# A decoder layer's ConvFFN: where modulation rows are fetched, how the first down weights are loaded, and the order at the turn of the down projection

## The chip, the core and the metric

The kernel runs on one core of one Trainium2 chip. The core has five engines, each with its own queue of instructions: TensorE (PE, matmuls; its weight loads are listed apart as PEld), VectorE (DVE), ScalarE (ACT), GpSimd (POOL) and SyncE (SP), which here only issues transfers. Sixteen DMA engines move data between HBM and the on-chip memory; transfers are issued by SP, by ACT and, for accumulating ones, by POOL. The metric is the device time of one execution in microseconds; lower is better.

## The reference

One layer on a sequence of 512 positions and 1024 channels in float32: a conditioned mixer (mLSTM heads and a Conformer convolution), then a conditioned ConvFFN. The change lies in the second half:

```
mod = silu(c) @ ada_w + ada_b          # six rows of 1024: sh1, sc1, g1, sh2, sc2, g2
...
u  = rms_norm(x, ffn_pre_g) * (1 + sc2) + sh2
up = causal_dwconv(u @ ffn_up, ffn_conv_w, ffn_conv_b)   # 1024 -> 2 * 2816, width 3
a, gt = split(up, 2)
f  = (silu(gt) * a) @ ffn_down                           # 2816 -> 1024
x  = x + g2 * rms_norm(f, ffn_post_g)
```

g2, the last of the modulation rows, is needed only at the end, and so its part of `mod` is computed late.

## The kernel before

**Products in two halves.** A float32 product is made of a high and a low half of each operand in the fast fp32r form: three matmuls, high by high, high by low, low by high (`mm3`, lines 188 to 190; `prod2`, line 1457). Halves are made in two ways. `split` lets ScalarE copy the high half (L1013) and VectorE subtract it (L1014). `added_split` (L1083 to L1085) lets ScalarE write the high half and its negative, and then GpSimd issues a software DMA that adds the source onto the negative, which leaves the low half: no VectorE work, but 256 KB of transfer with a landing to wait for. Halves live in a pool of 20 buffers, other tiles in 44 slots; raw weights arrive in two buffers of 128 x 2048 (`raws`), modulation rows in two of 128 x 1024 (`adas`).

**Up projection.** The 2816 gated channels are 22 blocks of 128 (`i`), taken in pairs, and a pair is one step `m`. From step 4 to step 10 (about 506 to 658 us) a step is one even block by a seven-product scheme of Strassen's kind (forms p1 to p7 of the weights' quarters, `weight_form`) and one odd block in the plain way, whose four quarters come from `value_part`, each an `added_split` (tiles wup_0, wup_1, wup_2, wup_3). Six quarter loads for the next step are issued by SP in the middle of a step. Steps 4 to 7 also fetch two blocks of modulation rows of 512 KB each on ACT's queue (`ada_fetch`) and sum them on VectorE against the conditioning vector (`ada_add`, L1148). `unit_out` multiplies the value by the gate into `F`.

**Down projection.** The same scheme, over 11 row blocks. Phase 1 (about 658 to 720 us) forms p1, p5, p7 and p6 from `b1`, `t1`, `t3`, `t2` (`load1`, `forms1`, `part_b`, `parts1`, `prod1`; `fh` and `fl` are the halves of the activations, in part reloaded from HBM). `b1` of the first blocks, and of the last three, is made by `added_split` (`part_b`), other halves by `split`. `t2` goes out to HBM and is read again. Then comes the turn: VectorE adds p6 and p1 into `su`, `su` into p5 and p7, and p7 into `sp5`, and TensorE goes on in the same banks with phase 2 (720 to 767 us), p2, p3 and p4, from `b2`, `b4`, `t4` (`load2`, `forms2`, `prod2`) and from the other activations `g2` (`forms_g2`). At the end the rows are normalised, scaled and written.

**What sets the order.** A scheduler orders each engine's instructions by what is ready; inside an `in_order()` block ScalarE, VectorE and GpSimd keep the order in which the code is written. SP's and TensorE's orders follow the code as well. Phase 1 and the up steps stand in such a block; phase 2 before the last products doesn't. There `behind_turn` keeps VectorE forms behind the instruction in `turn`, while `held` is true. A transfer waits on its issuing queue until its buffer is free, and holds up those behind it.

## Time and profile before

| what | value |
|---|---|
| timed runs | 773.89, 773.82, 771.59 us (median 773.82) |
| profiled execution | 775.42 us |
| its span, first to last instruction | 773.7 us |
| mean granted TensorE clock | 0.995 |
| TensorE busy | 755.8 us (98%) |
| VectorE busy | 643.5 us (83%) |
| ScalarE busy | 451.9 us (58%) |
| GpSimd busy | 370.8 us (48%) |
| bytes moved | 149.52 MB, 193 GB/s in the mean |

In the rows of a profile a matmul is busy until its modelled end, so that successive matmuls overlap: the distance of two starts, not the duration, is what one costs. A row of waits gives who waited, for whom, the total in us, how often, and the longest. A row of a tile gives the line, engine and operation, how many, the shortest, median and longest duration in ns, and the first and last start in us; "DMA to landing" is from issue to arrival. Names lose their numbers there: `p` stands for p1 to p7, `sp` for sp1 and sp5, `b_2l` for the low half of b1, b2 or b4 of block 2, `t_2l` likewise.

### The profile page before, as it was taken

The page shows a single profiled execution, that of the slowest core. Times are in us where ns is not written, and L with a number is a line of the kernel's source. Part 1 is how long each engine was busy: PE and PEld are TensorE (multiplying, and loading weights), DVE is VectorE, ACT ScalarE, POOL GpSimd, SP SyncE. Part 2 cuts the span into 40 slices and gives each one's busy share as a digit, 9 for nine tenths or more (in the row PEclk, how much of TensorE's full clock was granted, in tenths as well). Part 3 has the DMA queues.
Part 4 walks back from the last instruction along what each step waited for, and adds up shares of the span by engine and source line. Part 5 has one row for each costly group of instructions (what it writes and reads, how often), then busy time and mean ns, then how long its engine had stood idle before and what let it go on. Part 6 is the DMA issues. An engine that isn't in the chain of part 4 may idle for free.

```text
span 773.7 us, 11565 instructions
## 1 busy us (share of the span) xinstructions
PE 755.8 (98%) x3961; PEld 645.0 (83%) x3961; DVE 643.5 (83%) x1030; ACT 451.9 (58%) x864; POOL 370.8 (48%) x324
## 2 busy tenths in 40 slices
PE   7999999999999999999999999999998999899996
PEld 5888898778888888988889988899987989788785
DVE  6987999999999867746858589879898768996996
ACT  5447266776676356671344566676665657656662
POOL 2039587696797644452851445465555643100001
PEclk9999999999999999999999999999999999999998
DMA  9983214123031552436953678889988787999872
GB/s 328 383 287 133 84 55 170 75 74 118 28 116 75 168 194 75 164 108 226 346 189 143 186 190 208 244 214 238 219 210 201 173 235 185 283 361 359 315 259 108
DMA packets 56575, 149.52 MB, mean 193 GB/s; under 512 B 6434, under 2 KB 7874, under 8 KB 52420
## 3 DMA queue, kind: packets, MB, share of 16 engines
q1 hardware_dynamic: 33588, 100.37, 37.5%
q10 hardware_dynamic: 14288, 32.68, 12.2%
q0 software_dynamic: 8640, 15.73, 11.6%
q8 instruction: 31, 0.51, 0.3%
q14 instruction: 28, 0.23, 0.1%
HBM read 117.42 MB, written 15.61 MB: 172 GB/s over the span
## 4 chain that ended last, share of the span: by engine, by line
PE 52%; DVE 26%; DMA 13%; ACT 3%; issue 3%; POOL 1%; ACTq 0%; SPq 0%; DVEq 0%; POOLq 0%
DVE cv L731 10%; PE up L190 5%; PE up L189 5%; PE up L188 5%; PE p L1457 4%; PE glu L190 3%; PE glu L188 3%; PE glu L189 3%; DMA fh_1b<-own 2%; PE glu L316 2%; PE mixa L188 2%; PE mixa L190 2%; PE mixa L189 2%; PE mixb L190 2%; PE mixb L189 2%
## 5 line engine op out<-in xcount | busy, mean ns | idle before, releaser
L731 DVE SCALAR_TENSOR_TENSOR cv<-gt,cvw,cv 128x505 f32<-128x505 f32 (+24 forms) x200 | 137.3, 729 | 2.3 <-ACT cv L719 1.1
L727 POOL TENSOR_TENSOR cs<-cs,cs 128x510 f32<-128x510 f32 (+3 forms) x32 | 41.9, 1308 | 0.3
L725 ACT ACTIVATE cs<-gt,cvw 128x511 f32<-128x511 f32 (+4 forms) x40 | 27.4, 716 | 6.4 <-POOL cs L727 3.2
L685 POOL TENSOR_TENSOR ro2r<-ro2t,mhalf 128x1 f32<-128x1 f32 x1 | 0.6, 561 | 53.1 <-DVE ro2t L683 53.1
L189 PE MATMUL up<-u2l,wup_0h 128*128 128x512 f32 (+1 forms) x72 | 25.7, 356 | 0.2 <-DVE u2l L910 0.2
L188 PE MATMUL up<-u2h,wup_0h 128*128 128x512 f32 (+1 forms) x72 | 25.6, 356 | 0.0
L190 PE MATMUL up<-u2h,wup_0l 128*128 128x512 f32 (+1 forms) x72 | 25.5, 354 | 0.0
L171 POOL TENSOR_TENSOR wglu_0l<-wglu,wglu_0h 128x512 fp32r<-128x512 f32 x4 | 5.6, 1396 | 40.4 <-ACT wglu_0h L170 40.4
L171 POOL TENSOR_TENSOR wqko_1024l<-wqko,wqko_1024h 128x512 fp32r<-128x512 f32 x12 | 15.5, 1290 | 18.3 <-ACT wqko_1024h L170 12.9
L155 DVE SCALAR_TENSOR_TENSOR junk<-spare,cb 128x1024 bf16<-128x1024 f32 x12 | 19.0, 1586 | 3.6 <-DMA spare<-in_adaT 3.4
L155 DVE SCALAR_TENSOR_TENSOR junk<-ada,cb 128x1024 bf16<-128x1024 f32 x12 | 18.8, 1570 | 3.7 <-DMA ada<-in_adaT 3.6
L188 PE MATMUL qko<-uh,wqko_1024h 128*128 128x512 f32 x48 | 20.6, 430 | 0.0
L190 PE MATMUL up<-u2h,wup_2l 128*128 128x512 f32 x44 | 17.9, 408 | 2.7 <-DMA wup_2l<-wups 2.7
L188 PE MATMUL qko<-uh,wqko_0h 128*128 128x512 f32 x48 | 20.2, 420 | 0.0
L276 DVE SCALAR_TENSOR_TENSOR junk<-ada,cb 128x1024 bf16<-128x1024 f32 x16 | 19.5, 1220 | 0.1
L171 POOL TENSOR_TENSOR wo_512l<-wo,wo_512h 128x512 fp32r<-128x512 f32 x8 | 12.9, 1615 | 13.7 <-ACT wo_512h L170 13.7
L171 POOL TENSOR_TENSOR wqko_0l<-wqko,wqko_0h 128x512 fp32r<-128x512 f32 x12 | 16.6, 1386 | 5.0 <-ACT wqko_0h L170 4.9
L190 PE MATMUL qko<-uh,wqko_1024l 128*128 128x512 f32 x48 | 18.8, 392 | 0.0
L190 PE MATMUL qko<-uh,wqko_0l 128*128 128x512 f32 x48 | 18.8, 391 | 0.0
L171 POOL TENSOR_TENSOR wqko_512l<-wqko,wqko_512h 128x512 fp32r<-128x512 f32 x12 | 17.0, 1416 | 3.7 <-ACT wqko_512h L170 3.7
L171 POOL TENSOR_TENSOR wo_1024l<-wo,wo_1024h 128x512 fp32r<-128x512 f32 x8 | 11.6, 1454 | 14.9 <-ACT wo_1024h L170 14.9
L189 PE MATMUL qko<-ul,wqko_1024h 128*128 128x512 f32 x48 | 18.7, 390 | 0.0
(1247 smaller groups left out, 3136.9 us busy)
## 6 DMA issues: line engine op xcount, KB each, us to landing
wups<-in_w_up SPq DMA_DIRECT2D x56, 256.0 KB, 5.3
wqko<-in_w_qko SPq DMA_DIRECT2D x12, 1024.0 KB, 4.8
ada<-in_adaT ACTq DMA_DIRECT2D x20, 512.0 KB, 5.7
ada<-in_adaT SPq DMA_DIRECT2D x16, 512.0 KB, 6.8
wo<-in_w_out SPq DMA_DIRECT2D x8, 1024.0 KB, 4.8
wup<-in_w_up SPq DMA_DIRECT2D x8, 1024.0 KB, 6.1
spare<-in_adaT ACTq DMA_DIRECT2D x12, 512.0 KB, 7.4
wd<-in_w_down SPq DMA_DIRECT2D x20, 256.0 KB, 5.8
```

Source lines behind the costliest of these rows:

```text
L155: t = V.scalar_tensor_tensor(out=junk, in0=r, scalar=1.0, in1=cb, op0=ALU.mult, op1=ALU.mult, accum_out=mod[:, i : i + 1])
L171: (eng or G).tensor_tensor(out=lo[:, :n], in0=src, in1=hi[:, :n].bitcast(F32), op=ALU.subtract)
L188: PE.matmul(ps, a[0], b[0], start=start, stop=False)
L189: PE.matmul(ps, a[0], b[1], start=False, stop=False)
L190: PE.matmul(ps, a[1], b[0], start=False, stop=stop)
L276: V.scalar_tensor_tensor(out=junk, in0=first[k][:, i * D : (i + 1) * D], scalar=1.0, in1=cb, op0=ALU.mult, op1=ALU.mult, accum_out=part[k] ...
L316: PE.matmul(banks0[i], blk(wk, i)[a], u[k][b], start=k == 0 and a == b, stop=False)
L685: G.tensor_tensor(out=r, in0=t, in1=mhalf[:, :1], op=ALU.pow)
L725: S.activation(t[:, d:], cvx[j][:, : T - d], AF.Copy, scale=w(CK - 1 - d))
L727: G.tensor_tensor(out=side[:, d:], in0=side[:, d:], in1=t[:, d:], op=ALU.add)
L731: last_tap[0] = V.scalar_tensor_tensor(out=cp[:, d:], in0=cvx[j][:, : T - d], scalar=w(CK - 1 - d), in1=cp[:, d:], op0=ALU.mult, op1=ALU.add)
L1457: PE.matmul(ps[q], x, y, start=False, stop=m == NM - 1 and i == 2, skip_group_check=True)
```

## The change

Three things are done.

*Modulation rows.* `ada_fetch` goes from the step's start (behind the form p3, ahead of the six loads of quarters) to the place behind `value_part(j + 2, 0)`. Both `ada_add` go behind `unit_out`, where one stood ahead of it. ScalarE's queue around the fetch of one step, before (wup_p3h is the high half of the form p3; wup_2h and wup_2l are made for the plain block):

```order
L995 ACTIVATE fg9c<-up_1_5343,vec 128x512
L170 ACTIVATE wup_p3h<-s_5_5468 128x512
L1143 DMA ada_5487<-in_adaT 128x1024
L1143 DMA ada_5489<-in_adaT 128x1024
L1138 ACTIVATE fg9c<-fg9c 128x512
L1083 ACTIVATE wup_2h<-wups_5085 128x512
L1084 ACTIVATE wup_2l<-wups_5085 128x512
```

And now:

```order
L170 ACTIVATE wup_p5h<-wups_5084 128x512
L1084 ACTIVATE wup_0h<-wups_5085 128x512
L1085 ACTIVATE wup_0l<-wups_5085 128x512
L1144 DMA ada_5552<-in_adaT 128x1024
L1144 DMA ada_5554<-in_adaT 128x1024
L995 ACTIVATE fa10c<-upx_5392,vec 128x512
L995 ACTIVATE fg10c<-upz_5393,vec 128x512
```

The two fetches stood ahead of wup_2 of their step; they now stand behind wup_0 of the next block, in the second half of the step.

*Early down weights.* `load1(2)` becomes one load of 768 KB into a raw buffer, issued behind `forms1(0)`; block 3 stays raw, block 4 goes into four slots. `part_b(1)` goes ahead of the convolution fa21c. `part_b(10)` goes behind `parts1(9)`. SP's queue before:

```order
L1183 DMA wd_1_3_6693<-in_w_down 128x512
L1202 DMA t2d_4538<-wd_0b 128x512
L1183 DMA wd_2_1_6810<-in_w_down 128x512
L1183 DMA wd_2_2_6811<-in_w_down 128x512
L1183 DMA wd_2_3_6812<-in_w_down 128x512
L1179 DMA wd_3_6816<-in_w_down 128x1536
L1179 DMA wd_4_6818<-in_w_down 128x1536
```

And now:

```order
L1184 DMA wd_1_3_6693<-in_w_down 128x512
L1180 DMA wd_2_6763<-in_w_down 128x1536
L1203 DMA t2d_4538<-wd_0b 128x512
L1180 DMA wd_3_6811<-in_w_down 128x1536
L1184 DMA wd_4_1_6814<-in_w_down 128x512
L1184 DMA wd_4_2_6815<-in_w_down 128x512
L1184 DMA wd_4_3_6816<-in_w_down 128x512
```

Block 2's three loads stood behind the write of t2 of block 0 (`t2d`); its one load now stands ahead of that write.

*The turn.* The opening of phase 2 comes into the `in_order()` block. `forms2(0)` stands behind p1 of phase 1, `forms2(1)` is split: b2 behind the p5 sums, the rest behind the last sums. `forms2` of block 2 and above, and all of `forms_g2` there, are held behind the last low half of block 1. VectorE's queue before (`su`, `p`, `sp` are the sums; the number in b_2l is the block):

```order
L1014 TENSOR_TENSOR b_2l<-wdmore,b_2h 128x512
L1445 TENSOR_TENSOR p_0_6908<-p_0_6908,su_7460 128x512
L1014 TENSOR_TENSOR g2l_7596<-g2kept,g2h_7595 128x512
L1445 TENSOR_TENSOR p_1_6909<-p_1_6909,su_7461 128x512
L1014 TENSOR_TENSOR s_7597<-g2kept,s_7597 128x256
L1448 TENSOR_TENSOR p_0_6912<-p_0_6912,su_7460 128x512
L1014 TENSOR_TENSOR t_2l<-wdmore,t_2h 128x512
L1448 TENSOR_TENSOR p_1_6913<-p_1_6913,su_7461 128x512
L1450 TENSOR_TENSOR sp_0_7444<-p_0_6912,sp_0_7444 128x512
L1450 TENSOR_TENSOR sp_1_7445<-p_1_6913,sp_1_7445 128x512
```

And now, from the last of these sums to the first low half of block 2:

```order
L1447 TENSOR_TENSOR sp_1_7458<-p_1_6913,sp_1_7458 128x512
L1254 TENSOR_TENSOR wd_12_7378<-wd_12_7378 128x512
L1014 TENSOR_TENSOR b_1l<-wd_12_7378,b_1h 128x512
L1464 TENSOR_TENSOR sp_0_7457<-sp_0_7457,g2r 128x512
L1464 TENSOR_TENSOR sp_1_7458<-sp_1_7458,g2r 128x512
L1014 TENSOR_TENSOR t_1l<-wd_12_7378,t_1h 128x512
L1254 TENSOR_TENSOR wdmore<-wdmore 128x512
L1014 TENSOR_TENSOR g2l_7596<-g2kept,g2h_7595 128x512
L1254 TENSOR_TENSOR wdmore<-wdmore 128x512
L1254 TENSOR_TENSOR wd_15_7518<-wd_15_7518 128x512
L1014 TENSOR_TENSOR b_2l<-wdmore,b_2h 128x512
```

The forms of block 2, which alternated with the sums, all stand behind them, and behind what was held for block 1; the sums ahead of the first row shown stand together but for one low half of block 1. TensorE's and GpSimd's orders are as before.

```diff
@@ -1002,7 +1002,7 @@
     t2_d = [dram.tile([P, T], F32, tag=f"t2d{m}", name=f"t2d{m}") for m in range(NM)]
     pairs = []
 
-    turn, held = [], [False]
+    turn, held, newest = [], [False], []
 
     def behind_turn(op):
         if held[0]:
@@ -1011,7 +1011,8 @@
 
     def split(src, hi, lo):
         S.activation(hi, src, AF.Copy)
-        behind_turn(V.tensor_tensor(out=lo, in0=src, in1=hi.bitcast(F32), op=ALU.subtract))
+        newest[:] = [V.tensor_tensor(out=lo, in0=src, in1=hi.bitcast(F32), op=ALU.subtract)]
+        behind_turn(newest[0])
 
     def form_sums(m, F):
 
@@ -1163,7 +1164,7 @@
     loaded = {}
 
     def wd_raw(m, n):
-        return raws.tile([P, 2048], F32, tag="raw", name=f"wd{n}_{m}") if (m - 3) % 4 < 2 else more[:, m % 2, :]
+        return raws.tile([P, 2048], F32, tag="raw", name=f"wd{n}_{m}") if m == 2 or (m - 3) % 4 < 2 else more[:, m % 2, :]
 
     def parts(r, names):
         out = {}
@@ -1246,6 +1247,13 @@
         return [(h[:, :HT], l[:, :HT]), (h[:, HT:], l[:, HT:]), (s[:, :HT], s[:, HT:])]
 
     G2A = 3
+    def forms2(m, a=0, b=3):
+
+        r = loaded[m]
+        if b == 3:
+            behind_turn(V.tensor_tensor(out=r[2], in0=r[0], in1=r[2], op=ALU.subtract))
+        return parts(r, [(f"b2_{m}", 0), (f"b4_{m}", 1), (f"t4_{m}", 2)][a:b])
+
     def opening_products(m):
         for which in ("p1", "p5", "p7", "p6"):
             if m == 1 and which == "p7":
@@ -1281,7 +1289,6 @@
 
     with in_order():
         i = 2 * MS
-        fetched = [ada_fetch(40 + n) for n in range(2)]
         a11, a12, a21, a22 = places(i)
         weight_form(i, "p1", a11)
         V.tensor_tensor(out=a11, in0=a11, in1=a21, op=ALU.subtract)
@@ -1310,8 +1317,6 @@
             bj, ba, bg = before
             bg = conv3(bg, NF + bj, f"fg{bj}")
             weight_form(i, "p3", s4)
-            if MS < m < MS + 4:
-                fetched = [ada_fetch(40 + 2 * (m - MS) + n) for n in range(2)]
             if more_to_come:
                 for n, q in ((i, 2), (i, 0), (j, 0), (i, 3), (j, 1), (i, 1)):
                     up_load(n + 2, (q,))
@@ -1321,6 +1326,7 @@
             between(i, *banks)
             if not more_to_come:
                 forms1(0)
+                load1(2)
             gate.append(value_part(j, 3))
             if more_to_come:
                 up_load(j + 2, (2, 3))
@@ -1334,25 +1340,24 @@
             if m == NM - 1:
                 wide = adas.tile([P, D], F32, tag="ada", name="g2r")
                 g2.append(row(3, lambda n: [wide[:, :T], wide[:, T:]], "g2"))
-            ada = [(40 + 2 * (m - MS) + n, fetched[n]) for n in range(2)] if m < MS + 4 else []
             if more_to_come:
                 weight_form(i + 2, "p1", a11)
                 V.tensor_tensor(out=a11, in0=a11, in1=a21, op=ALU.subtract)
                 V.tensor_tensor(out=a21, in0=a21, in1=a22, op=ALU.add)
             else:
                 part_b(0)
+                part_b(1)
             va = conv3(pa, j, f"fa{j}")
             if not more_to_come:
                 parts1(0)
                 forms1(1)
-                part_b(1)
-                load1(2, [slot(f"wd1_2_{b}") for b in range(4)])
-                for n in (3, 4):
-                    load1(n)
+                load1(3)
+                load1(4, [slot(f"wd1_4_{b}") for b in range(4)])
             if more_to_come:
                 weight_form(i + 2, "p7", a11)
                 weight_form(i + 2, "p5", a21)
                 value = [value_part(j + 2, 0)]
+                ada = [(n, ada_fetch(n)) for n in range(40 + 2 * (m - MS), 42 + 2 * (m - MS))] if m < MS + 4 else []
                 V.tensor_tensor(out=a11, in0=a22, in1=a11, op=ALU.subtract)
             if m - 1 < SPILLED:
                 own_out(m - 1)
@@ -1365,10 +1370,8 @@
             if more_to_come:
                 weight_form(i + 2, "p6", a11)
                 value.append(value_part(j + 2, 1))
-            for n, r in ada[:1]:
-                ada_add(n, r)
             unit_out(i, vx, vz, Fs[m])
-            for n, r in ada[1:]:
+            for n, r in ada:
                 ada_add(n, r)
             if m == MS + 4:
                 ada_done(40, 48)
@@ -1396,9 +1399,9 @@
             forms1(m)
             if m < 6 or NM - G2A <= m < NM - 1:
                 part_b(m)
+            parts1(m)
             if m == NM - 2:
                 part_b(NM - 1)
-            parts1(m)
             if m + 3 < NM:
                 load1(m + 3)
             if 4 <= m < 4 + SPILLED:
@@ -1417,37 +1420,36 @@
             if m < M1:
                 for which in ("p1", "p5", "p7", "p6"):
                     prod1(m, which)
+        w2 = {}
+        for which in ("p1", "p5", "p6", "p7"):
+            for m in range(M1, NM):
+                prod1(m, which)
+            if which == "p1":
+                sp1 = [slot(f"sp1_{q}") for q in range(2)]
+                for q in range(2):
+                    S.activation(sp1[q], p1[q], AF.Copy)
+                w2[0] = forms2(0)
+            elif which == "p5":
+                sp5 = [slot(f"sp5_{q}") for q in range(2)]
+                for q in range(2):
+                    S.activation(sp5[q], p5[q], AF.Copy)
+            elif which == "p6":
+                su = [slot(f"su_{q}") for q in range(2)]
+                for q in range(2):
+                    V.tensor_tensor(out=su[q], in0=p6[q], in1=sp1[q], op=ALU.add)
+                for q in range(2):
+                    V.tensor_tensor(out=p5[q], in0=p5[q], in1=su[q], op=ALU.add)
+                w2[1] = forms2(1, 0, 1)
+            else:
+                for q in range(2):
+                    V.tensor_tensor(out=p7[q], in0=p7[q], in1=su[q], op=ALU.add)
+                for q in range(2):
+                    V.tensor_tensor(out=sp5[q], in0=p7[q], in1=sp5[q], op=ALU.add)
+                w2[1] |= forms2(1, 1, 3)
+                turn.append(newest[0])
     g2r = g2[0]
 
-    def forms2(m):
-
-        r = loaded.pop(m)
-        behind_turn(V.tensor_tensor(out=r[2], in0=r[0], in1=r[2], op=ALU.subtract))
-        return parts(r, [(f"b2_{m}", 0), (f"b4_{m}", 1), (f"t4_{m}", 2)])
-
-    w2, g2 = {}, g2f
-    for which in ("p1", "p5", "p6", "p7"):
-        for m in range(M1, NM):
-            prod1(m, which)
-        if which == "p1":
-            sp1 = [slot(f"sp1_{q}") for q in range(2)]
-            for q in range(2):
-                S.activation(sp1[q], p1[q], AF.Copy)
-        elif which == "p5":
-            sp5 = [slot(f"sp5_{q}") for q in range(2)]
-            for q in range(2):
-                S.activation(sp5[q], p5[q], AF.Copy)
-        elif which == "p6":
-            su = [slot(f"su_{q}") for q in range(2)]
-            for q in range(2):
-                V.tensor_tensor(out=su[q], in0=p6[q], in1=sp1[q], op=ALU.add)
-            for q in range(2):
-                V.tensor_tensor(out=p5[q], in0=p5[q], in1=su[q], op=ALU.add)
-        else:
-            for q in range(2):
-                V.tensor_tensor(out=p7[q], in0=p7[q], in1=su[q], op=ALU.add)
-            for q in range(2):
-                turn.append(V.tensor_tensor(out=sp5[q], in0=p7[q], in1=sp5[q], op=ALU.add))
+    g2 = g2f
 
     def prod2(m, which, q):
         a12, a22, s4 = g2[m]
@@ -1462,11 +1464,11 @@
         V.tensor_tensor(out=sp5[q], in0=sp5[q], in1=g2r[1], op=ALU.mult)
     xrs = []
     for m in range(NM):
+        held[0] = True
         if m >= G2A:
-            held[0] = m > G2A
             g2[m] = forms_g2(m)
-        held[0] = m >= G2A
-        w2[m] = forms2(m)
+        if m > 1:
+            w2[m] = forms2(m)
         if M2 - NT <= m < M2:
             tt = m - M2 + NT
             xrs.append([cvtile(f"xr{tt}_{hf}") if tt < 2 else slot(f"xr{tt}_{hf}") for hf in range(2)])
```

## The prediction

> **What bounds the kernel now.** I read the page first, then the waits of TensorE, then its stretches, and last the tiles for which it waited.
>
> From the page, the span and the engines, and then TensorE's two longest waits from 520 us to the end (us in total, times, longest):
>
> ```profile
> span 773.7 us, 11565 instructions
> PE 755.8 (98%) x3961; PEld 645.0 (83%) x3961; DVE 643.5 (83%) x1030; ACT 451.9 (58%) x864; POOL 370.8 (48%) x324
> PE up L190 <- DMA wup_2l<-wups: 2.7, 2, 2.2
> PE p L189 <- DMA b_1l<-wd: 1.9, 1, 1.9
> ```
>
> TensorE is the bound (98% busy), so only its idle time and its clock can give anything; the change touches nothing before 506 us. Behind these two come only two waits for VectorE sums, of 0.24 and 0.39 us (part C shows them); each of the four names a transfer or a sum that the change moves. What the stretches say (us; busy us and instructions of TensorE, its weight loads, VectorE, ScalarE, GpSimd; granted clock, DMA share, GB/s):
>
> ```profile
> 564.00:585.00 21.00, 20.50 (x130) 18.57 (x130) 17.59 (x27) 13.03 (x24) 11.67 (x11) 1.00 0.85 212
> 588.00:592.00 4.00, 3.89 (x10) 3.06 (x11) 3.93 (x7) 3.05 (x7) 2.58 (x3) 0.57 0.79 186
> 660.00:665.00 5.00, 3.06 (x14) 2.23 (x13) 4.90 (x9) 3.38 (x7) 0.88 (x1) 1.00 1.04 371
> 700.00:720.00 20.00, 20.00 (x88) 16.28 (x88) 13.24 (x22) 14.01 (x27) 0.87 (x1) 1.00 1.04 356
> 720.00:740.00 20.00, 19.32 (x83) 15.03 (x82) 20.00 (x37) 11.96 (x26) 0.00 (x0) 1.00 0.85 299
> ```
>
> After the longest wait the clock was 0.57 from 588 to 592 us: the missing 0.43 of 4.00 us is 1.7 us. The same did not follow the 1.9 us wait near 662 us (clock 1.00). Losses within reach: 2.7 + 1.7 + 1.9 + 0.6 = 6.9 us. From 700 to 720 us the DMA engines are full, and VectorE is full from 720 to 740 us; both matter below.
>
> **Part A, the modulation rows.** Two fetches of 512 KB per step leave the step's start, where five weight loads are issued too, and go behind the quarter-0 value of the next unit; both sums that read them go behind the gating product. What waits now is the low half wup_2l, which software DMA accumulates. Its issue and landing (us) in the step of 577 us, which has a fetch, and in two steps without:
>
> ```profile
> L1085 POOL DMA_DIRECT2D wup_2l<-wups x1: 897/897/897, 577.3 to 577.3; - x1
> DMA to landing us min/median/max: 10.7/10.7/10.7
> L1085 POOL DMA_DIRECT2D wup_2l<-wups x2: 887/887/887, 599.6 to 620.6; - x2
> DMA to landing us min/median/max: 5.1/5.2/5.3
> ```
>
> Without a fetch it lands 5.4 us sooner; the longest lateness is 2.2 us (the other wait on it, 0.5 us, is in the step before). So all 2.7 us go, and with them the 1.7 us at the low clock: 4.4 us. The Trainium skill (TensorE: Matmul & The Clock Gate, Part 1: The HAM clock gate) says that the clock is halved after at least one idle window of about 3.4 us; here an idle of 2.2 us was enough, so the trace speaks against that number. By that rule no wait of this kernel costs clock, and part A would be worth 2.7 us.
>
> What comes due in the fetch's new place? The low half wup_0l goes out just ahead of it, wup_1l and wup_p2l follow, and the sums wait for the rows (the landing is that of all fetches):
>
> ```profile
> L1085 POOL DMA_DIRECT2D wup_0l<-wups x1: 911/911/911, 542.2 to 542.2; - x1
> L190 PE MATMUL up<-u2h,wup_0l x4: 389/389/389, 554.1 to 556.2; 128*128 128x512 f32 x4
> L1148 DVE SCALAR_TENSOR_TENSOR junk<-ada,cb x4: 1214/1218/1222, 524.6 to 547.4; 128x1024 bf16<-128x1024 f32 x4
> DMA to landing us min/median/max: 3.7/6.8/9.8
> L1110 DVE TENSOR_TENSOR u<-upx,p x1: 417/417/417, 555.4 to 555.4; 128x256 f32<-128x256 f32 x1
> L1092 PE MATMUL upx<-u2h,wup_p2h x4: 278/283/283, 559.1 to 560.2; 128*128 128x256 f32 x4
> ```
>
> wup_0l has 554.1 - 542.2 = 11.9 us; with 10.7, the worst landing seen under a fetch, it still comes 1.2 us early. The fetch is now issued near 541.3 (behind the wup_0l activation, about 0.9 us ahead of that row), and the last sum of a step starts at 547.4. A fetch took 3.7 to 9.8 us over the program, so the rows are there between 545.0 and 551.1: VectorE waits 0 to 3.7 us. Behind the waiting sums stand the forms of the next step on VectorE; the nearest one for TensorE ends at 555.4 + 0.4 = 555.8 and is wanted at 559.1, 3.3 us later. TensorE thus pays 0 to 0.4 us, and I take 0. Part A: -4.4 us (0 to -4.4, if the load only moves on to another low half).
>
> Each DMA engine takes turns between its queues by packets, says the Trainium skill (DMA: Bandwidth & Descriptors, Queues, rings and completion order). By that rule the fetch slows whatever stands beside it, wherever it is put, which agrees with 10.7 against 5.1 to 5.3.
>
> **Part B, the early down weights.** load1(2) becomes one raw load right behind the first forms; part_b(1) goes ahead of the convolution fa21c; part_b(10) goes behind parts1(9). ScalarE now (start, us), the landing of b_1l, and VectorE's waits after 636 us:
>
> ```profile
> 648.85 0.76 ACT L995 ACTIVATE fa21c<-up,vec 128x512 f32<-128x512 f32 x1
> 651.08 0.62 ACT L1083 ACTIVATE b_1h<-wd 128x512 fp32r<-128x512 f32 x1
> L1085 POOL DMA_DIRECT2D b_1l<-wd x1: 895/895/895, 652.6 to 652.6; - x1
> DMA to landing us min/median/max: 11.7/11.7/11.7
> DVE t_5l L1014 <- ACT t_5h L1013: 1.0, 2, 0.7
> ```
>
> b_1h starts near 648.85 instead of 651.08, so the accumulation starts 2.2 us earlier (I take 2.0), and 768 KB of loads leave its neighbourhood. It landed at 664.3; TensorE waited 1.9 us. 2.0 us cover that: -1.9 us.
>
> The price is fa21c 1.1 us later (two activations at a pitch of 0.52 us), and VectorE's convolution and forms behind it. VectorE has its next waits at t_5l, 1.0 us in all, which came with slots that TensorE frees; it takes the 1.1 back there to 0.1. TensorE does not see it, since each b of this stage comes from GpSimd.
>
> But TensorE then runs 1.9 us earlier into a full DMA, and the last low half does not come earlier. Load of m=10 (KB, us to landing), then b_10:
>
> ```profile
> L1179 SPq DMA_DIRECT2D wdmore<-in_w_down x1: 382/382/382, 693.4 to 693.4; - x1
> wdmore<-in_w_down SPq DMA_DIRECT2D x1, 768.0 KB, 8.8
> 702.26 0.63 ACT L1083 ACTIVATE b_10h<-wdmore 128x512 fp32r<-128x512 f32 x1 [4.25 <-PE p L189]
> L1085 POOL DMA_DIRECT2D b_10l<-wdmore x1: 872/872/872, 703.8 to 703.8; - x1
> DMA to landing us min/median/max: 6.9/6.9/6.9
> L189 PE MATMUL p<-b_10l,fh_0b x2: 397/448/499, 710.8 to 711.6; 128*128 128x512 f32 x2
> PEld p L189: 0.3, 1
> ```
>
> The load lands at 693.4 + 8.8 = 702.2, just where b_10h starts: freeing TensorE's slot sooner does not help. b_10l lands at 703.8 + 6.9 = 710.7, and TensorE, which wants it at about 710.5 now, will want it at 708.6. It waits 2.1 us there, 1.9 more than now. That is the old wait in a new place: between 0 (everything lands 1.9 sooner) and 3.0 (the 1.1 us of VectorE is not taken back). A wait of this size stands between the one that cost clock and the one that did not; I take no clock loss, with 1.7 us as the other end. Part B: -1.9 + 1.9 = 0 (-1.9 to +2.8).
>
> **Part C, the turn.** VectorE now (start, duration) and the TensorE starts around it:
>
> ```profile
> 720.00 0.39 PE L190 MATMUL p<-t_10h,fl_0b 128*128 128x512 f32 x1
> 722.42 0.69 DVE L1445 TENSOR_TENSOR p<-p,su 128x512 f32<-128x512 f32 x1
> 723.02 0.68 DVE L1014 TENSOR_TENSOR g2l<-g2kept,g2h 128x512 fp32r<-128x512 f32 x1
> 723.62 0.69 DVE L1445 TENSOR_TENSOR p<-p,su 128x512 f32<-128x512 f32 x1
> 723.74 0.39 PE L1457 MATMUL p<-b_0h,s 128*128 128x512 f32 x1
> 724.37 0.50 PE L1457 MATMUL p<-b_0h,s 128*128 128x512 f32 x1 [0.24 <-DVE p L1445]
> 726.08 0.39 PE L1457 MATMUL p<-b_1l,s 128*128 128x512 f32 x1
> 726.31 0.39 PE L1457 MATMUL p<-b_1h,s 128*128 128x512 f32 x1
> 727.09 0.50 PE L1457 MATMUL p<-t_0h,g2h 128*128 128x512 f32 x1 [0.39 <-DVE sp L1450]
> ```
>
> Sums and low halves alternate at 0.60 us each. TensorE's steady pitch is 726.31 - 726.08 = 0.23 us; the two pauses cost 0.63 - 0.23 = 0.40 and 0.78 - 0.23 = 0.55 us. In the written order the su and p5 sums come before p7 is complete, and the four sums after TensorE's last p7 product (720.23) stand together: they end at 720.2 + 4 x 0.60 + 0.1 = 722.7, before either pause. So 0.95 us go. The price is that all of m=2 now comes behind the turn. By the order, ten VectorE rows stand between the last sum and the first low half of m=2, itself included: 722.7 + 10 x 0.60 = 728.7, its end at 728.8. TensorE has the products of m=0 and m=1 ahead of it, 36 matmuls from 720.23 on: 720.23 + 36 x 0.227 = 728.4. So 0.4 us of new wait; 0.2 if the low half counts only as the product's second matmul, and 1.6 if the two products behind the squares of ScalarE wait two passes of 0.60. Part C: -0.95 + 0.4 = -0.55 us (-0.75 to +0.65).
>
> **Sum.** -4.4 + 0 - 0.55 = -4.95 us, from the profiled execution's 775.42 us (span 773.7 and 1.7 around it): 770.5. The median of the timed runs, 773.82, is 1.6 below that execution. Either profiling costs 1.6, then the timed run gives 768.9, or timed runs lack some of these waits, then 770.5; I take 769.6 (0.9 below).
>
> **The rivals.**
> 1. All waits go: b_10l comes early as well, since 768 KB left the crowd. 775.42 - 4.4 - 1.9 - 0.75 = 768.4, less 0.9: 767.5. For it: the load at 643 us meets idle queues. Against: the DMA share of 1.04 from 700 to 720 us.
> 2. The wait moves to b_10l and the clock falls: 769.6 + 1.7 = 771.3. For it: 2.2 us did that once. Against: 1.9 us did not.
> 3. The fetch moves its crowd to wup_0l or wup_1l in one step, which then costs what 585 us costs now, 2.2 + 1.7 = 3.9: 769.6 + 3.9 = 773.5, no change. For it: the DMA share of the steps is 0.85. Against: 1.2 us in hand at the worst landing.
> 4. Slower, the same mechanism in two steps or more: 769.6 + 2 x 3.9 = 777.4. It decides from the point where an accumulation beside the fetch's new place takes over 11.9 us. For it: the rows are fetched in four steps, all alike. Against: no accumulation here took over 11.7, and that one stood at a share of 1.04.
>
> **How the numbers follow.** The forecast, 769.6, has a chance of 0.48, with its own range of 768.0 to 771.3; rival 1 has 0.20, rival 2 0.17, rival 3 0.10, rival 4 0.05. The range that should hold the time 8 times in 10 takes in the forecast, rival 1 down to 1 us below its time (the 1.6 us of profiling and the slow restarts behind each wait, which the sum leaves out) and rival 2 up to 1 us above: 766.3 to 772.4. A measurement of this kernel can tell 0.3%, 2.3 us: faster is below 771.5. The forecast, rival 1 and 0.12 of rival 2 lie there: 0.80; no change is the other 0.05 of rival 2 and rival 3: 0.15; slower is 0.05.
>
> **What would show it.** Right for A: no wait for wup_2l, the clock at 1.00 around 588 us, and the end of the last up step 4 us earlier. Right for B: no wait for b_1l, and a wait of about 2 us on b_10l. Right for C: the sums in one run on VectorE, and under 0.5 us of waits for m=2. Wrong: a wait on wup_0l, wup_1l or the rows; no wait on b_10l (rival 1); a clock under 1.00 behind it (rival 2).

## The result, and the profile after

The changed kernel takes 781.1 us (median of 4 runs, 779.45 to 782.52) against 773.75 us before: 1.0101 times, 95% interval 1.0071 to 1.0131. It is slower, where 769.6 us was forecast. Its profiled execution, the fastest of the four, took 779.45 us (span 777.7), 4.0 us more than that of before, so that the two traces hold 4.0 of the 7.35 us between the medians. Two of the other three runs had a mean granted clock of 0.993 in place of 0.996; what else they lost, no trace shows. In the experiments below the kernel before was timed again beside each kernel (medians of 774.85 to 775.52 us, 25 to 31 runs), and each ratio is to those runs.

TensorE's waits from 500 us on in the changed kernel (us in total, times, longest):

```profile
PE p L189 <- DMA b_10l<-wdmore: 2.6, 1, 2.6
PE p L189 <- DMA b_5l<-wdmore: 1.7, 1, 1.7
PE upx L1093 <- ACT fh L1030: 1.7, 2, 0.9
PE p L1459 <- DVE t_10l L1014: 0.8, 1, 0.8
PE upx L1093 <- DVE upx L1113: 0.7, 1, 0.7
PE p L1459 <- DVE t_9l L1014: 0.5, 1, 0.5
```

None of the four old waits is left: wup_2l, b_1l and the two sums are in time. Six other rows stand in their place, 8.0 us in all. The stretches of the changed kernel (us; busy us and instructions of TensorE, weight loads, VectorE, ScalarE, GpSimd; clock, DMA share, GB/s):

```profile
588.00:592.00 4.00, 4.00 (x19) 3.33 (x18) 3.93 (x5) 3.23 (x6) 3.43 (x4) 1.00 0.83 236
660.00:665.00 5.00, 5.00 (x24) 4.14 (x23) 4.90 (x9) 3.38 (x7) 0.88 (x1) 1.00 0.84 283
683.00:687.00 4.00, 2.27 (x10) 1.60 (x9) 2.63 (x5) 0.31 (x1) 0.00 (x0) 1.00 1.07 355
709.00:717.00 8.00, 5.37 (x17) 3.96 (x16) 4.70 (x8) 3.87 (x8) 0.00 (x0) 0.79 1.06 372
756.00:762.00 6.00, 4.71 (x20) 3.23 (x19) 3.62 (x8) 2.54 (x6) 0.19 (x1) 1.00 0.01 3
```

The two old holes, near 588 and 662 us, are full now. The new ones are at 684, at 709 (2.6 us idle, then a clock of 0.79 over the 8 us: 1.7 us of full clock gone) and at 757 us. Three waits of VectorE in the changed kernel that the kernel before lacks:

```profile
DVE su L1439 <- PE p L190: 3.1, 1, 3.1
DVE fa21c L997 <- ACT fa21c L995: 2.9, 1, 2.9
DVE b_0l L1014 <- ACT b_0h L1013: 2.1, 1, 2.1
```

TensorE runs the same 3961 matmuls in the same order in both kernels, so the start of one matmul in the two traces says what has been won or lost up to it:

| matmul | before, us | after, us | after - before | lies behind |
|---|---|---|---|---|
| p2 of the step at 582 us | 582.12 | 583.92 | +1.80 | three waits at p2, less a shorter wait at the first wup_2l |
| wup_1h of the next step | 604.01 | 601.68 | -2.33 | no more wait and half clock at wup_2l |
| b_0l, phase 1 | 658.16 | 656.93 | -1.23 | one more wait at p2 |
| t_2h | 675.13 | 671.66 | -3.46 | no more wait at b_1l |
| b_8h | 704.14 | 702.73 | -1.42 | the wait at b_5l |
| b_0l, phase 2 | 720.46 | 723.38 | +2.92 | the wait at b_10l and the half clock |
| t_0h, phase 2 | 727.66 | 729.04 | +1.39 | no more pauses for the sums |
| t_9h, phase 2 | 755.12 | 757.37 | +2.25 | five losses of about 0.16 us at low halves of blocks 2 and 3 |
| the last one | 766.56 | 770.61 | +4.05 | the waits at t_9l and t_10l |

TensorE was 3.46 us ahead at 671 us, and 4.05 us behind at the end.

### The profile page after: what moved, and what is told of

The parts are those of the page before. It is cut to its first block, busy times and chain, and to the rows that moved or that the text cites. A ratio compares the mean times of both kernels' runs of the same rounds, so it can differ in the third digit from the quotient of the medians.

```text
span 777.7 us, 11564 instructions
## 1 busy us (share of the span) xinstructions
PE 757.8 (97%) x3961; PEld 645.3 (83%) x3961; DVE 643.7 (83%) x1030; ACT 449.3 (58%) x864; POOL 370.6 (48%) x324
## 4 chain that ended last, share of the span: by engine, by line
PE 55%; DVE 29%; DMA 8%; issue 3%; ACT 3%; ACTq 1%; SPq 0%; POOL 0%; DVEq 0%; POOLq 0%
DVE cv L731 10%; PE up L189 5%; PE up L188 5%; PE up L190 5%; PE glu L316 3%; PE glu L190 3%; PE glu L189 3%; PE glu L188 3%; PE upx L1093 2%; DVE junk L1149 2%; PE mixa L188 2%; PE mixa L190 2%; PE mixa L189 2%; PE mixb L188 2%; PE mixb L189 2%
## 5 line engine op out<-in xcount | busy, mean ns | idle before, releaser
L189 PE MATMUL qko<-ul,wqko_0h 128*128 128x512 f32 x48 | 18.7, 390 | 0.0
L190 PE MATMUL qko<-uh,wqko_512l 128*128 128x512 f32 x48 | 18.7, 389 | 0.0
```

The lines of the kernel that those rows point to most:

```text
L189: PE.matmul(ps, a[0], b[1], start=False, stop=False)
L190: PE.matmul(ps, a[1], b[0], start=False, stop=stop)
```

## The experiments on the modulation rows

**The part alone.** The edit is that part of the diff.

> The kernel before with the change of the modulation rows alone (fetches late, both sums behind the gating product). Theory 1 (each part keeps in isolation what the two traces show of it): matmuls of the last up step start 1.2 us earlier than before, since 4.9 us of wait and clock at wup_2l go and about 3 us of waits for VectorE at the product p2 come; the time falls by about 1 us or, if the earlier start only meets the later transfers, by 0. Theory 2 (the late sums cost more than the fetch gives, and the gain came from other parts): slower by 1 us or more. The step of the prediction (nothing comes back on VectorE): faster by 4 us.

776.65 us, 1.0021 times the time before (1.0002 to 1.0040). Its waits for wup_2l are gone; in their place, in the profile of this run:

```profile
PE upx L1092 <- ACT fh L1029: 1.7, 2, 0.9
PE upx L1092 <- DVE upx L1112: 0.9, 1, 0.9
```

**One sum left in its place.**

```diff
+                ada = [(n, ada_fetch(n)) for n in range(40 + 2 * (m - MS), 42 + 2 * (m - MS))] if m < MS + 4 else []
...
             for n, r in ada[:1]:
                 ada_add(n, r)
             unit_out(i, vx, vz, Fs[m])
             for n, r in ada[1:]:
                 ada_add(n, r)
```

> As the run with the modulation rows alone, but one of the two sums stays ahead of the gating product, as before; only the fetches move. Theory 1 (the waits at p2 come from the two sums standing together behind the gating product, which leaves VectorE idle 0.8 us and puts 1.3 us more behind it): no waits at p2 over 0.3 us, the last up step 3.5 to 4.5 us earlier than before. Theory 2 (the rows land late in the new place and VectorE waits for them): the waits at p2 stay, and VectorE shows waits for the rows.

771.82 us, 0.9955 times (0.9936 to 0.9974): faster. TensorE's list of waits from 500 us on has one row:

```profile
PE p L189 <- DMA b_10l<-wdmore: 2.4, 1, 2.4
```

No wait at p2, none for wup_2l, and 0.2 us of VectorE for the rows. The matmul that starts at 648.16 us before starts at 643.58. Against the profile of before the late fetch alone thus gives a little more than the 4.4 us that the prediction put on it (by the starts 4.9: this run is 0.33 us behind the kernel before at 549 us, and 4.58 ahead at 604). By the medians it gives 3.4 us (771.82 against 775.21). The wait at wup_2l is not the same in each execution, which accounts for the difference. Nine of the kernels profiled here have the code of before in these steps (that kernel, and all below that leave the modulation rows alone). TensorE lost 2.2 to 4.9 us in them at wup_2l, by the starts against this run, 3.4 in the mean and most in the profile of before; the clock fell there in two of the nine. With the turn alone, for instance, the wait was longer than before, and the clock stayed at 1.00 around the longer of its two parts:

```profile
PE up L190 <- DMA wup_2l<-wups: 3.8, 2, 2.9
```

```profile
584.00:594.00 10.00, 7.10 (x42) 5.93 (x41) 8.66 (x11) 6.08 (x11) 5.64 (x5) 1.00 0.87 218
```

The place of the first sum takes about as much as the fetch gives, 3.3 us (lost at p2 in the run ahead of this one: 0.23, 1.07, 1.03 and 1.00).

Why, shows VectorE in one step. First the kernel before (start, duration), then the changed one, with GpSimd's row:

```profile
524.62 1.22 DVE L1148 SCALAR_TENSOR_TENSOR junk<-ada,cb 128x1024 bf16<-128x1024 f32 x1
525.76 0.69 DVE L1139 TENSOR_TENSOR F<-fa8c,fg8c 128x512 f32<-128x512 f32 x1
526.37 1.22 DVE L1148 SCALAR_TENSOR_TENSOR junk<-ada,cb 128x1024 bf16<-128x1024 f32 x1
527.51 2.37 DVE L1307 TENSOR_TENSOR s<-wups 128x512 f32<-128x512 f32 x1
529.80 1.52 DVE L997 SCALAR_TENSOR_TENSOR fg9c<-up,vec,fg9c 128x511 f32<-128x511 f32 x2
```

```profile
526.90 0.69 DVE L1140 TENSOR_TENSOR F<-fa8c,fg8c 128x512 f32<-128x512 f32 x1 [0.76 <-ACT fg8c L1139]
527.51 1.22 DVE L1149 SCALAR_TENSOR_TENSOR junk<-ada,cb 128x1024 bf16<-128x1024 f32 x1
528.77 3.08 DVE L1149 SCALAR_TENSOR_TENSOR junk<-ada,cb 128x1024 bf16<-128x1024 f32 x1
531.78 0.68 DVE L1314 TENSOR_TENSOR s<-wups 128x512 f32<-128x512 f32 x1
529.12 1.63 POOL L171 TENSOR_TENSOR wup_p4l<-wups,wup_p4h 128x512 fp32r<-128x512 f32 x1
```

The first sum stood in the time in which VectorE waits for ScalarE's gate. Behind the product it leaves that time empty. From the end of the convolution fg8c (524.71 us before, 526.14 now) to the start of the next, fg9c (529.80 and 532.39), VectorE took 5.09 us before and takes 6.25 now, 1.16 more. 0.76 us of this are the empty time. Some 0.2 us come from the row that runs beside GpSimd's wup_p4l (from 527.70 us before, 529.12 now) and is the long one in both kernels: before it was `s`, 2.37 us in place of the 0.68 that it takes now, and now it is the second sum, 3.08 in place of 1.22. The rest is short pauses. This chain has no rest in which to take it back: it feeds p2 of the next step.

**Both sums late, the fetches early.**

```diff
-            for n, r in ada[:1]:
-                ada_add(n, r)
             unit_out(i, vx, vz, Fs[m])
-            for n, r in ada[1:]:
+            for n, r in ada:
                 ada_add(n, r)
```

> The kernel before with one edit: both sums over modulation rows behind the gating product; the fetches stay at the step's start. Theory 1 (the place of the sums alone makes the waits at p2): waits at p2 of about 1 us in three steps, the waits at wup_2l as before or shorter (what is late anyway hides the rest), the end of the up steps 0 to 3 us later than before. Theory 2 (the waits at p2 come from the late fetch): no wait at p2 over 0.3 us.

777.56 us, 1.0030 times (1.0010 to 1.0051). Neither theory had its form: there is no wait at p2, yet the end of the up steps is 1.5 us later than before. TensorE lost 6.4 us between 500 and 604 us by the starts, where the nine kernels with the code of before lost 2.2 to 4.9; all but 0.2 us of it at wup_2l. In the step at 557 us its accumulation was issued 3.2 us later than in the profile of before (554.5), with TensorE 0.9 us later:

```profile
L1085 POOL DMA_DIRECT2D wup_2l<-wups x1: 887/887/887, 557.7 to 557.7; - x1
```

That row alone proves little: in one of the nine kernels, the one with b_10l's accumulation late (below), it stands at 557.5 us too. That the place of the sums costs by itself, the time and the 6.4 us show; by which way the lateness comes to wup_2l is not shown.

**The mended place in the changed kernel.** This edit taken back there:

```diff
+            for n, r in ada[:1]:
+                ada_add(n, r)
             unit_out(i, vx, vz, Fs[m])
-            for n, r in ada:
+            for n, r in ada[1:]:
                 ada_add(n, r)
```

> The changed kernel with one edit: one of the two sums over modulation rows stays ahead of the gating product. Theory 1 (the sums' place is what costs in part A, and the rest is independent of it): no wait at p2 over 0.5 us, TensorE 3 us earlier at the end of the up steps, 2 to 3.5 us faster than the changed kernel, that is about 1.005 to 1.007 times the kernel before. Theory 2 (the stretch of full DMA up to the turn swallows what comes ahead of it): the waits at b_5l and b_10l grow by the 3 us and the time stays at 1.009 or more.

777.46 us, 1.0034 times (1.0011 to 1.0056), against 1.0101 unmended. The end of the up steps comes 3.8 us earlier than in the changed kernel, and TensorE's last matmul 5.3 us earlier in the profiled executions. That is more than expected; the wait at b_10l was 1.5 us here and cost no clock, that at b_5l did.

## The experiments on the down weights

**The part alone** is all of the diff on `wd_raw`, `load1` and `part_b`. Then the same **with b_1 behind the convolution**:

```diff
                 part_b(0)
-                part_b(1)
             va = conv3(pa, j, f"fa{j}")
             if not more_to_come:
+                part_b(1)
                 parts1(0)
```

> The kernel before with the change of the down weights alone. Theory 1 (ScalarE gives fa21c 1.5 us late, VectorE never takes it back, and so the weights of blocks 5 and 10 land late, while TensorE comes early): no wait at b_1l (1.9 gone), a wait of 1.5 to 3 us at b_10l, perhaps with the clock halved behind it; time the same to 3 us slower. Theory 2 (the loss at b_10l in the changed kernel came from part A making TensorE early): wait at b_10l under 1 us, time 1 to 2 us faster.

> The down weights alone, but with the two activations of block 1's b behind the convolution fa21c and ahead of t_0, in place of ahead of fa21c. Theory 1 (VectorE's chain is set back by fa21c, and this lateness is carried to the weights of blocks 5, 8 and 10): VectorE's wait for fa21c falls from 3.2 to 2 us or less, b_5l's wait from 2.0 to under 1 us, b_10l lands about 1 us earlier, time 1 us below that of the part alone. Theory 2 (the raw load of 768 KB and the fuller queues are what holds the chain): the wait for fa21c stays above 2.5 us or moves to another row, and the time stays.

778.65 us, 1.0044 (1.0025 to 1.0064), and 777.05 us, 1.0015 (0.9994 to 1.0037). In the first VectorE waits 3.2 us for fa21c, TensorE 2.0 us at b_5l and 2.4 at b_10l; in the second 1.8 us, nothing at b_5l, and 1.9 at b_10l, but 1.6 at b_0l. So theory 1 holds by these rows (the intervals of the two times overlap), and half of the set-back is still there. What is the rest?

**The loads alone**, early, and then the same loads at the old place:

```diff
+                load1(2)          # early: behind forms1(0); late: just ahead of load1(3)
...
-                load1(2, [slot(f"wd1_2_{b}") for b in range(4)])
-                for n in (3, 4):
-                    load1(n)
+                load1(3)
+                load1(4, [slot(f"wd1_4_{b}") for b in range(4)])
```

> The loads of blocks 2, 3 and 4 alone (one early raw load of 768 KB, raw, four slots); the low halves of blocks 1 and 10 in their old places. Theory 1 (the early load makes ScalarE's own transfer issues longer, and these hold fa21c): the two g2r issues take 2.2 us or more in place of 1.1, VectorE waits 1 to 2 us for fa21c, and the time is 0 to 2 us slower. Theory 2 (only the two activations ahead of fa21c cost): the issues take 1.1 us, no wait for fa21c over 1 us, the same time or faster.

> As the loads of blocks 2, 3 and 4 alone, but the raw load of block 2 stands behind the write of t2 of block 0, where its three loads stood before: the same bytes, buffers and sizes, issued near 650 us in place of 643 us. Theory 1 (the 768 KB in flight make ScalarE's g2r issues long, and these hold b_0 and fa21c): the issues take 1.1 us again, fa21c is waited for under 1 us, b_10l lands 1.2 us or more earlier, reckoned from the end of the up steps, than with the early load. Theory 2 (the buffers, not the time of the load, set the chain back): the issues take 1.1 us, but the chain is late all the same and b_10l lands within 0.5 us of the run with the early load.

Early: 776.76 us, 1.0019 (0.9993 to 1.0045). Late: 773.55 us, 0.9990 (0.9970 to 1.0010). The intervals overlap; what follows rests on the rows. ScalarE issues two transfers (g2r) just ahead of b_0h. Their rows in the changed kernel, with the early load alone, and with the late one:

```profile
645.86 2.34 ACTq L663 DMA_DIRECT2D g2r<-row_d  x2
```

```profile
645.53 2.52 ACTq L663 DMA_DIRECT2D g2r<-row_d  x2
648.10 0.63 ACT L1083 ACTIVATE b_0h<-wd 128x512 fp32r<-128x512 f32 x1 [3.21 <-DVE wd_0b L1191]
```

```profile
646.01 1.11 ACTq L663 DMA_DIRECT2D g2r<-row_d  x2
647.16 0.63 ACT L1083 ACTIVATE b_0h<-wd 128x512 fp32r<-128x512 f32 x1 [1.36 <-DVE upz L1113]
```

With 768 KB just issued, these two issues hold ScalarE for 2.3 and 2.5 us in place of 1.1, and b_0 and fa21c, in the changed kernel b_1 too, stand behind them. It is the time of the load: the same bytes and buffers later don't do it.

What this sets back shows in one measure: the time from the first product of phase 1 (the first start of b_0h) to the issue of b_10l. For the two runs with the loads:

```profile
L188 PE MATMUL p<-b_0h,fh x2: 388/393/398, 656.4 to 658.2; 128*128 128x512 f32 x2
L1085 POOL DMA_DIRECT2D b_10l<-wdmore x1: 869/869/869, 703.9 to 703.9; - x1
```

```profile
L188 PE MATMUL p<-b_0h,fh x2: 388/392/395, 657.3 to 658.0; 128*128 128x512 f32 x2
L1085 POOL DMA_DIRECT2D b_10l<-wdmore x1: 872/872/872, 703.3 to 703.3; - x1
```

| kernel | first b_0h, us | issue of b_10l, us | between |
|---|---|---|---|
| before | 657.9 | 703.8 | 45.9 |
| fetches and sums; fetches with one sum ahead | 658.4; 653.4 | 704.1; 699.1 | 45.7; 45.7 |
| sums late alone | 659.4 | 705.6 | 46.2 |
| turn alone; turn filled | 658.0; 658.9 | 703.8; 704.8 | 45.8; 45.9 |
| turn filled, fetches with one sum ahead | 655.5 | 701.2 | 45.7 |
| loads at the old place | 657.3 | 703.3 | 46.0 |
| loads early | 656.4 | 703.9 | 47.5 |
| down weights, b_1 behind fa21c | 655.0 | 702.6 | 47.6 |
| down weights alone | 655.6 | 704.5 | 48.9 |
| all three parts; with one sum ahead | 656.7; 652.9 | 705.0; 702.0 | 48.3; 49.1 |

Some 46 us wherever the early load is absent, whether TensorE waited at b_1l or not; 1.5 us more with it, and about 1 us more again with the two activations ahead of fa21c. Phase 1 can't end ahead of that issue and its landing, 7 us later.

**The accumulation of b_10l behind block 9's other halves**, alone:

```diff
+            parts1(m)
             if m == NM - 2:
                 part_b(NM - 1)
-            parts1(m)
```

> One edit alone: the accumulation of b_10l behind the other halves of block 9. Theory 1 (b_10h waits for its load, not for TensorE or for its place in the order): b_10l lands within 0.5 us of the time that the load allows, wait at b_10l as before plus what TensorE is early, the same time within 1 us. Theory 2 (the later place itself makes b_10l late): b_10l lands 1 us or more later behind its load than before, 1 to 3 us slower.

775.87 us, 1.0008 (0.9986 to 1.0030); 45.7 us between b_0h and the issue. Theory 1: this piece is without effect.

## The experiments on the turn

**The part alone**, and **with all forms of block 1 ahead of the sums**:

```diff
                 w2[0] = forms2(0)
+                w2[1] = forms2(1)
...
-                w2[1] = forms2(1, 0, 1)
...
-                    V.tensor_tensor(out=sp5[q], in0=p7[q], in1=sp5[q], op=ALU.add)
-                w2[1] |= forms2(1, 1, 3)
-                turn.append(newest[0])
+                    turn.append(V.tensor_tensor(out=sp5[q], in0=p7[q], in1=sp5[q], op=ALU.add))
```

> The kernel before with the turn alone. Theory 1 (the written order leaves VectorE idle at the turn, while it is the bound of phase 2, and the idle time comes back at the last low halves t_9l and t_10l): the waits for the sums go (0.6), VectorE is idle over 2 us between 710 and 722 us, its last low half comes 1 to 4 us later, and the time is 0.5 to 3 us slower. Theory 2 (the idle time in the changed kernel was due to b_10l alone): VectorE is idle under 1.5 us there, and the time is 0.5 to 1.5 us faster.

> The turn alone, but with all forms of block 1 ahead of the sums in place of between and behind them, so that VectorE has them to do while it waits for p6; the turn point is the last sum. Theory 1 (idle VectorE at the turn comes back at the end): idle time ahead of the first sum under 1 us in place of 2.4, its last low half about 2 us earlier than in the run with the turn alone, the waits at t_9l and t_10l mostly gone, and the time 1 to 2.5 us below that run. Theory 2 (the late forms come from the holding of block 2 and above behind the turn, whatever stands ahead): the waits at the end stay at 1.5 us or more.

778.42 us, 1.0020 (1.0000 to 1.0040), and 775.95 us, 0.9998 (0.9977 to 1.0020). In the part alone VectorE waits ahead of the first sum, and TensorE at the end for VectorE (the waits of the one and of the other):

```profile
DVE su L1444 <- PE p L190: 2.4, 1, 2.4
```

```profile
PE p L1464 <- DVE t_10l L1014: 0.8, 1, 0.8
PE p L1464 <- DVE t_9l L1014: 0.6, 1, 0.6
```

Filled, the wait ahead of the first sum is 0.15 us and both waits at the end are gone from TensorE's list, which holds only wup_2l (2.8) and b_10l (2.2). The loss at t_9l and t_10l falls from 2.00 to 0.37 us, reckoned from the starts. Theory 1: the four rows of block 1 that stand behind the sums in the written order are work that VectorE could do while it waits for p6, and phase 2 has too little room for them later. The two times are 2.5 us apart in the median, as theory 1 had it at most, but their intervals overlap: the rows carry this, not the times.

## The experiments on b_10l

b_10l is the wait that all of these meet, so its low half was made by VectorE instead:

```diff
         for m in range(3, NM):
+            if m == NM - 1:
+                w1[m] = parts(loaded[m], [(f"b1_{m}", 1)])
             forms1(m)
...
-            if m == NM - 2:
-                part_b(NM - 1)
```

> The kernel before with one edit: the low half of b1 of block 10 is made by VectorE (split, just ahead of that block's forms) and not by an accumulating transfer. Theory 1 (the landing of b_10l near 711 us sets the end of phase 1; what is won ahead of it is lost there): no wait at b_10l, its low half ready near 703 to 705 us, and TensorE's last matmul 1.5 to 2.5 us earlier than in a run where b_1l was in time; the time 0 to 2.5 us faster. Theory 2 (VectorE has no room there, and phase 2 is bound by it): its low halves of phase 2 come later by the 0.6 us and the time is the same or slower.

> Late fetches with one sum ahead of the gating product, and b_10l made by VectorE. Theory 1 (landing of b_10l): the 2.6 us lost at b_10l and the 1.6 us of low clock behind it in the run without this edit go, TensorE's last matmul near 758 to 760 us in place of 762.2; the time 2 to 4 us below that run, 5.5 to 8 us faster than the kernel before. Theory 2 (VectorE becomes the bound of phase 2): waits for t_9l, t_10l or b of block 2 appear and half or more of it is given back; 3 to 5 us faster than before.

On the kernel before: 773.72 us, 0.9985 (0.9966 to 1.0005). With the late fetches and one sum ahead: 771.88 us, 0.9958 (0.9932 to 0.9983), the same as without it. The wait at b_10l is gone, phase 2 begins 4.8 us earlier than before, and the next thing is late; TensorE's longest wait in the first run is

```profile
PE p L1457 <- DVE p L1445: 1.7, 2, 1.5
```

in place of 0.2: the sums, which alternate with the low halves. So these were put together with the filled turn, without and with b_10l by VectorE:

> Late fetches with one sum ahead of the gating product, and the turn with the forms of block 1 ahead of the sums; the down weights as before. Theory 1 (the gain of the fetch moves everything behind it, and the waiting at b_10l takes part of it): last matmul 1 to 2 us earlier than with the fetches alone, since the sums' pauses stay away; wait at b_10l 2 to 2.5 us; 4 to 6 us faster than before. Theory 2 (phase 2 is bound by VectorE and gives it back): the same time as with the fetches alone, 3.5 us faster.

> As the run with late fetches and the filled turn, and b_10l made by VectorE. Theory 1 (landing of b_10l is the last thing that holds TensorE before the turn): no wait at b_10l, none at the sums, the last matmul at 758 to 760 us, 6 to 8 us faster than before. Theory 2 (transfers bound the stretch from 660 us to the turn, so that TensorE meets the next late one): a wait of 1.5 us or more for forms of phase 2 or for the sums, and at most 1 us faster than without this edit.

772.59 us, 0.9972 (0.9953 to 0.9990), and 771.04 us, 0.9954 (0.9933 to 0.9975). Theory 2 for the last: no wait at b_10l or at the sums, but at forms of phase 2, early and late:

```profile
PE p L1459 <- DVE t_10l L1014: 0.8, 1, 0.8
PE p L1459 <- DVE t_2l L1014: 0.5, 1, 0.5
PE p L1459 <- DVE b_3l L1014: 0.5, 1, 0.5
PE p L1459 <- DVE t_9l L1014: 0.2, 1, 0.2
```

VectorE waits there itself for t2, read back from HBM (5.1 us in this run). Whether those reads or VectorE's own work bound phase 2 was not told apart. The best two versions, 0.9954 and 0.9955, beat both kernels; the second is one moved fetch.

## Why the prediction was wrong

Alone, the three parts cost 1.6, 3.4 and 1.6 us by their ratios (1.0021, 1.0044, 1.0020), where -4.4, 0 and -0.55 us were forecast; together that is 0.85 of the 1.01% that was measured. (The intervals of the first and the last reach down to 1.0002 and 1.0000.)

**Part A.** The step that failed is "TensorE thus pays 0 to 0.4 us, and I take 0". It asked only whether the rows land in time (they did: with one sum in place VectorE waited 0.2 us for them in all), and took the 3.3 us between the form's end and p2 as free. It left out that the first sum had filled a wait. Behind the product the wait stays empty, and VectorE's chain is 1.16 us longer in such a step, with no rest from step to step. Measured: 3.1 us lost at p2 in the changed kernel (0.24, 0.86, 1.01, 1.02 by the starts). The term for the fetch, -4.4, was on the high side: 3.4 us by the medians (2.0 to 5.0 by the interval). It was read from one execution, the dearest of nine, and a loss of clock like its 1.7 us came in only two of them; that the run with one sum in place agrees with it in the traces is luck of that execution.

**Part B.** b_1l came in time as said (-2.2 us). Failed: "it takes the 1.1 back there to 0.1". fa21c was waited for 2.9 us, not 1.1, for the early load made ScalarE's issues long. The 1.0 us of waits at t_5l did go, but VectorE then waited 1.7 us at b_6l in place of 0.5, so that on balance nothing was taken back: b_10l was issued 48.3 us behind b_0h, not 45.9. Failed too: "TensorE does not see it, since each b of this stage comes from GpSimd". (b_6 and b_7 do not.) GpSimd's issue waits for ScalarE's halves, and these stand in ScalarE's order behind halves of forms that VectorE makes: t_4h starts right behind VectorE's second form of block 4, at 674.30 us in place of 672.82, and b_5h behind t_4h at 675.89 in place of 675.10. So b_5l landed at 686.0 us (issued at 677.4, 8.6 to landing) in place of 684.3, and TensorE, 3.5 us ahead, waited 1.7 us for it, which wasn't foreseen. The new wait at b_10l was named, with 2.1 us; it was 2.6, and the clock fell behind it, as rival 2 had it (1.7 us). Also the premise was weak. Without the early load, b_1l's wait was 0 to 0.2 us in the runs with the fetches alone, with one sum ahead, with the turn alone, filled, and with b_10l's accumulation late, and b_10l's was 1.9 to 2.4 in each. So the 1.9 us of the profile before was not a loss of its own: where it is missing, the wait at b_10l appears.

**Part C.** The pauses went (1.5 us by the starts; 0.95 was forecast, since a third pause of 0.21 us and the slow starts behind each were left out). The sums stood as forecast behind the last p7 products, and ended at 725.5 us in place of 722.7 only because TensorE came there 2.9 us late, from b_10l. Failed: "So 0.4 us of new wait". It asked what stands behind the sums only up to block 2, and put VectorE's idle time ahead of the sums at nothing: 3.1 us of waiting for TensorE's p6. VectorE was busy all of the 20 us from 720 us on and 14.9 of the next 17, so that this time returned: five losses of about 0.16 us at blocks 2 and 3, and 1.9 us at t_9l and t_10l. With the filled turn all but 0.37 us of such losses is gone. A wait of 0.8 us of VectorE for t2 of the last block, read back from HBM, stands just ahead of t_9l; as in the last run above, the part of these reads was not told apart.

**The rivals.** The slower side came, with a chance of 0.05, but not by rival 4's mechanism: wup_0l was never late. The range had no case in which VectorE's lateness is carried through a whole phase.

## What to carry to other kernels

Ahead of moving work on an engine, ask what idle time it fills now: an instruction that stands in a wait costs little there, and 1 us away it leaves the wait empty and the chain longer (here by 1.16 us), and again in every step if the chain feeds the next one. Before a wait is counted as a gain, follow the next late thing behind it on a chain that doesn't depend on it (here the issue of b_10l, 45.7 to 46.2 us behind b_0h in nine kernels): what is won ahead of that point is lost there. And a wait seen in one execution may be one of two places where the same lateness can fall, or, as at wup_2l, one draw of a size that goes from 2.2 to 4.9 us: compare several profiles ahead of making it a term of a sum.

## What was not expected of the hardware

An issue of a transfer on ScalarE is not of constant length: the two g2r issues took 1.1 us, and 2.3 to 2.65 in each of the runs with 768 KB issued about 3 us ahead on SP's queue. The trace doesn't show what the issuing engine waits for.

Whether a wait costs TensorE its clock is not set by its length alone. Over 8 us around the wait at b_10l, in the run with the sums late and the fetches early:

```profile
709.00:717.00 8.00, 5.56 (x25) 4.28 (x24) 6.72 (x12) 6.55 (x13) 0.00 (x0) 1.00 1.06 369
```

It idles 2.4 us there with the clock at 1.00; the changed kernel idles 2.6 us in the same stretch, and its row, shown with the result, has 0.79. Waits of 1.9 us went both ways (0.79 in the run with the turn alone, 1.00 with fetches and sums), the wait of 2.9 us at wup_2l shown above cost no clock, and each drop cost another 1.6 to 1.7 us. The Trainium skill (TensorE: Matmul & The Clock Gate, Part 1: The HAM clock gate) has the activity counted in free-running windows of some 3.4 us, in which case it would matter where a wait falls in its window; the scatter agrees with that, but 1.9 us were enough here, less than the idle window that the page asks for.
